# A two-block transformer layer on one core: modulation rows summed along the free axis on VectorE instead of across partitions on GpSimd

## The chip, the core and the metric

The kernel runs on one core of a Trainium2 chip. The engines are TensorE (PE: matmuls; PEld: its weight loads), VectorE (DVE), ScalarE (ACT), GpSimd (POOL) and SyncE (SP), which issues all DMAs of this kernel, in order, from one queue. The metric is the device time of one execution, in microseconds (us).

## The reference

A sequence of 256 tokens with 1024 features goes through two blocks in float32. The first has a hybrid attention mixer, a memory attention and a SwiGLU feed-forward (FFN, 2816 wide); the second is a block whose two norms are modulated by a conditioning vector c:

```python
mod = silu(c) @ w_ada + b_ada                 # c: 1 x 1024, w_ada: 1024 x 6144
shift_m, scale_m, gate_m, shift_f, scale_f, gate_f = split(mod, 6)
h = rms(x) * (1 + scale_m) + shift_m
x = x + gate_m * (mixed(h @ w_in) @ w_out)    # forgetting attention and retention
h = rms(x) * (1 + scale_f) + shift_f
x = x + gate_f * (relu(h @ w_mlp_in)**2 @ w_mlp_out)
```

Block 1 is, in short, `h += merged @ w_out`, where `merged` sums three gated up-projections; `h += memory_attention(h)`; `h += swiglu(rmsnorm(h))`; and a final norm. All six rows of `mod` depend on c alone, so they can be worked out at any time before block 2 needs them.

## The kernel before

**Products.** Every weight comes in tiles of 128x1024 float32 (512 KB; a tile `raw` takes one slot of a pool of 37). ACT rounds it to a high part `wh`, VectorE makes the low part `wl = raw - wh`, and TensorE adds three products of high and low parts in PSUM (`ps`). Activations are brought into the transposed layout as `aT` (or `hT`), by ACT for the high part and VectorE for the low part. In the merge, `mg` is the sum of gated up-projections and `mgt` a gated summand.

**Order.** The whole program is first recorded as operations, then a planner (`Plan`) with a cost for each operation lists them engine by engine in the order in which its model finds them ready; that order is fixed in the program, and each engine runs its own list in order. All instructions are issued from one helper, so they all bear its line, L646 (L634 in the changed kernel); rows are told apart by tile names. The planner's model knows GpSimd's software library: an all-reduce and the other GpSimd work need different ones, and going from one to the other costs `RELOAD`.

**Modulation.** `modulation()` makes s = silu(c) as a 128x8 tile: feature p*8+j lies in partition p, column j. `mod_part(q)` works out half a row of `mod` (512 columns), for q from 0 to 11: GpSimd clears an accumulator `mod` (128x512), a DMA puts 512 values of b_ada into its partition 0, four DMAs bring 512 KB of w_ada each (as `raw`), VectorE does eight products, accumulator += raw times column j of s (`mod_s` in the rows); GpSimd's `partition_all_reduce` sums over the 128 partitions; for the two scale rows VectorE adds 1; a DMA stores 512 values in a DRAM tile `mod_rows`. `mod(i)` later reads row i back, broadcast to all partitions, as `modrow`.

Four parts are started between the products of the merge (`MODG`), six between the groups of the FFN (`MODF`), two in the second block's MLP. Five rows are read back near the FFN's end, the last in the MLP.

The root of a norm is a power on GpSimd, a tensor_tensor of `s` with `mhalf`; `xn` on VectorE, the normed input, waits for it.

Of the kernel before, what the change touches and what calls it, by code (L numbers as in the profile page):

```python
# [16 lines left out]
ALU = mybir.AluOpType  # L17
# [3 lines left out]
P = 128  # L21
S = 256
NT = 2
DM = 1024
# [83 lines left out]
CUTS = ((0, 512, 1024), (0, 512, 768, 1024))  # L108
PIECES = ((0, 256, 512, 1024), (0, 256, 512, 768, 1024))
PIECES0 = ((0, 256, 512, 1024), (0, 512, 1024))  # L110
HORIZON, WINDOW, RELOAD = 30.0, 140, 6.5
TUNING = [
    (1.5, 8.0, 0.1, 5.0, (('qc', 1), ('va_qb', 2))),
    (1.5, 8.0, 0.0, 1.0, (('stick', 8),)),
# [159 lines left out]
class Plan:  # L274
# [146 lines left out]
    @staticmethod  # L421
    def cost(o, views):
        if not views:
            return 1.29
        n = max(math.prod(v.shape[1:]) for v in views)
        psum = any(v.root.kind == "ps" for v in views)
        if o.eng == "pe":
            if o.name == "transpose":
                return 0.11
            n, dt = math.prod(o.args[0].shape[1:]), o.args[1].dtype  # L430
            one = max(0.109, n / 600) if dt == F32 else max(0.054, n / 2250)
            return one * (0.6 if dt == F32 and o.args[0].shape[0] in (32, 64) else 1.0) + 0.0043
        if o.eng == "act":
            return (0.051 if psum else 0.094) + n / 1200 + 0.093 * (isinstance(o.kw.get("scale"), View)
                                                                    + isinstance(o.kw.get("bias"), View) + ("accum_out" in o.kw))
        if o.eng == "dve":
            if o.name == "reciprocal":
                return 0.07 + 0.0062 * n
            fast = not psum and o.name in ("tensor_copy", "tensor_scalar")
            small = o.name in ("tensor_scalar", "scalar_tensor_tensor") and len(views) > (2 if fast else 3)  # L440
            return 0.068 + n / (1920 if fast else 960) + 0.06 * small
        if o.eng == "pool":
            if o.name == "partition_all_reduce":
                return 3.57
            if o.name == "memset":
                return 0.035 + n / 1200
            if ALU.pow in o.args:
                return 0.3 + 0.165 * n
            return 0.15 + n * (0.0034 if o.name == "tensor_scalar" else 0.0031 if o.name == "tensor_copy" else 0.0021)
        return Plan.moved(o)  # L450
# [42 lines left out]
    def begin(self):  # L493
        s = State()
# [5 lines left out]
        s.left = [len(o.pred) for o in self.ops]  # L500
        s.form, s.start, s.end = ([None] * len(self.ops) for _ in range(3))
        s.avail = {e: [] for e in self.HOP}
        s.order, s.library = [], False
        s.clock["pool"] = 8.3
        for o in self.ops:
            if not o.pred:
                self.offer(s, o)
# [2 lines left out]
    def offer(self, s, o):  # L510

        for f in o.forms:
# [2 lines left out]
                e = s.form[q.i][0]  # L515
                at = max(at, s.end[q.i] + self.LAG[e].get(f[0], self.LAG[e][None]))
            s.avail[f[0]].append((o, f, at))

    @staticmethod
    def foreign(s, name):  # L520

        return name != "memset" and (name == "partition_all_reduce") != s.library

    def run(self, s, keys, wait, patience, stop):

# [21 lines left out]
        while len(s.order) < len(ops) and s.dense < stop:  # L547
            best = None
            for e, av in s.avail.items():
                t0 = max(s.clock[e], s.now)  # L550
                cand = []
                for c in av:
                    o, f, ready = c
                    at = room(o, e, t0)
                    if e == "pool" and at is not None and self.foreign(s, f[1]):
                        at = max(at, s.clock[e] + RELOAD)
                    if at is None:
                        continue
                    t = max(t0, ready, at)
# [20 lines left out]
                continue  # L580
            t, e, (o, f, _) = best
            i = o.i
            if e == "pool" and self.foreign(s, f[1]):
                s.library = not s.library
            s.start[i], s.form[i] = t, f
            for r in o.roots:
                if r.kind in todo and s.slot[r.i] is None:
# [61 lines left out]
class Net:  # L649
# [1048 lines left out]


    def modulation(self):  # L1700
        nc, a = self.nc, self.a
        self.mod_w = a["w_ada_2"].rearrange("(p j) n -> p j n", p=P)
        self.mod_rows = self.tile("dram", DM, nm="mod_rows")[0:6]
        c, s = (self.fixed(8, f"mod_{n}") for n in "cs")
        nc.sync.dma_start(c, a["c_2"].rearrange("a (p j) -> (a p) j", p=P))
        nc.vector.tensor_scalar(s, c, -80.0, None, ALU.max)
        nc.scalar.activation(s, s, AF.Exp, scale=-1.0)
        nc.vector.tensor_scalar(s, s, 1.0, None, ALU.add)
        nc.vector.reciprocal(s, s)
        nc.vector.tensor_tensor(s, s, c, ALU.mult)  # L1710
        self.mod_c = s

    def mod_part(self, q):

        nc = self.nc
        c0 = q * 512
        acc = self.k(2, [P, 512], nm="mod")
        nc.gpsimd.memset(acc, 0.0)
        nc.sync.dma_start(acc[0:1, :], self.a["b_ada_2"][:, c0:c0 + 512])
        for j0 in range(0, 8, 2):  # L1720
            raw = self.k(4, [P, 1024], nm="raw")
            r = raw.rearrange("p (k n) -> p k n", k=2)
            nc.sync.dma_start(r, self.mod_w[:, j0:j0 + 2, c0:c0 + 512])
            yield
            for j in range(2):
                nc.vector.scalar_tensor_tensor(acc, r[:, j, :], self.mod_c[:, j0 + j:j0 + j + 1], acc, ALU.mult, ALU.add)
        yield
        nc.gpsimd.partition_all_reduce(acc, acc, channels=P, reduce_op=bass_isa.ReduceOp.add)
        if q // 2 in (1, 4):
            yield  # L1730
            nc.vector.tensor_scalar(acc, acc, 1.0, None, ALU.add)
        yield
        nc.sync.dma_start(self.mod_rows[q // 2:q // 2 + 1, c0 % DM:c0 % DM + 512], acc[0:1, :])

    def next_part(self):
        if not self.mod_parts:
# [407 lines left out]
def views(aps):  # L2144

    out = {}
    for k, ap in aps.items():
        if k in ("b_ada_2", "c_2", "norm_final", "const_a", "const_b"):
            out[k] = ap
        else:  # L2150
            out[k] = ap[0]
    return out


# [17 lines left out]
```

## Time and profile before

| | |
|---|---|
| Time, median of 3 runs | 784.13 us (782.67 to 786.28) |
| Profiled execution | 782.47 us |
| Its span in the profile | 780.7 us |
| TensorE busy | 751.6 us (96%) |
| VectorE busy | 603.6 us (77%) |
| ACT busy | 395.6 us (51%) |
| GpSimd busy | 95.4 us (12%) |
| Read from HBM | 159.22 MB, 205 GB/s over the span |

The span reaches from the first to the last instruction; the time of an execution has some 1.8 us more. Busy means that an instruction runs; a busy TensorE can run at the full clock (granted clock 1.00) or at half of it (0.50). "Idle before" is the time an engine stood still ahead of an instruction, with what released it. SPq is SP's DMA queue.

### The profile page before, as it was taken

How to read it: one execution, taken by the hardware profiler on the slowest of the kernel's cores; microseconds unless marked ns; L12 is line 12 of the kernel's file. 1: busy time of each engine (PE TensorE's matmuls, PEld its weight loads, DVE VectorE, ACT ScalarE, POOL GpSimd, SP SyncE). 2: the span in 40 equal slices, each digit the busy share in tenths (PEclk: the TensorE clock that was granted, in tenths of full speed). 3: DMA queues.
4: the chain of work that ended last, by engine and by line, in shares of the span. 5: the costliest groups of instructions: out<-in, count | busy, mean ns of one | idle time of the engine just before them, and what ended most of it. 6: DMA issues, size and time to landing. Idle time of an engine off the chain costs nothing. (4 is left out here: it accounts for less than half of the span.)

```text
span 780.7 us, 13305 instructions
## 1 busy us (share of the span) xinstructions
PE 751.6 (96%) x5195; PEld 683.7 (88%) x5195; DVE 603.6 (77%) x933; ACT 395.6 (51%) x652; POOL 95.4 (12%) x75
## 2 busy tenths in 40 slices
PE   5999999997998999999999899999999999999998
PEld 4978899996897999999999678798887999999996
DVE  5999989989589997877827788889769997555522
ACT  6684774346278645333326464663536535544510
POOL 0112002411000112222200122020101021000000
PEclk9999999998999999999999999999999999999999
DMA  9828475957366686788788576635427886555401
GB/s 315 268 82 256 157 234 186 362 211 248 135 213 226 210 276 230 239 283 268 243 291 253 151 211 161 142 108 195 156 82 270 288 299 236 188 181 187 159 1 55
DMA packets 92019, 161.17 MB, mean 206 GB/s; under 512 B 6227, under 2 KB 42227, under 8 KB 91956
## 3 DMA queue, kind: packets, MB, share of 16 engines
q1 hardware_dynamic: 91956, 160.32, 62.5%
q8 instruction: 41, 0.67, 0.4%
q14 instruction: 22, 0.18, 0.1%
HBM read 159.22 MB, written 1.07 MB: 205 GB/s over the span
## 5 line engine op out<-in xcount | busy, mean ns | idle before, releaser
L646 DVE TENSOR_TENSOR wl<-raw,wh 128x1024 fp32r<-128x1024 f32 (+4 forms) x237 | 298.5, 1289 | 65.5 <-ACT wh L646 55.2
L646 ACT ACTIVATE wh<-raw 128x1024 fp32r<-128x1024 f32 (+4 forms) x237 | 243.1, 1042 | 161.4 <-DMA raw<-in_w_ffn_out_dram 30.5
L646 PE MATMUL ps<-aT,wh 128*128 128x256 f32 x1664 | 307.1, 284 | 0.6 <-ACT silu L646 0.6
L646 PEld LDWEIGHTS ps<-aT,wh 128*128 128x128 f32 x1664 | 258.1, 189 | 2.0 <-issue 1.0
L646 PE MATMUL ps<-aT,wl 128*128 128x256 f32 x832 | 236.1, 284 | 0.0
L646 PE MATMUL ps<-wh,aT 128*128 128x512 f32 (+5 forms) x672 | 185.1, 360 | 7.1 <-ACT aT L646 5.2
L646 PEld LDWEIGHTS ps<-aT,wl 128*128 128x128 f32 x832 | 157.1, 189 | 0.1
L646 PE MATMUL ps<-wh,hT 128*128 128x512 f32 (+1 forms) x540 | 142.1, 352 | 3.0 <-ACT hT L646 2.4
L646 PEld LDWEIGHTS ps<-wh,aT 128*128 128x128 f32 x672 | 120.2, 192 | 24.8 <-ACT aT L646 5.9
L646 PE MATMUL ps<-wl,aT 128*128 128x512 f32 (+5 forms) x336 | 118.6, 357 | 0.0
L646 PEld LDWEIGHTS ps<-wh,hT 128*128 128x128 f32 x540 | 94.8, 190 | 18.2 <-ACT hT L646 2.9
L646 PE MATMUL ps<-wl,hT 128*128 128x512 f32 (+1 forms) x270 | 94.8, 351 | 0.0
L646 DVE SCALAR_TENSOR_TENSOR mod<-raw,mod_s,mod 128x512 f32<-128x512 f32 x96 | 71.9, 749 | 6.5 <-DMA raw<-in_w_ada_dram 5.0
L646 POOL PARTITION_ALL_REDUCE mod<-mod x12 | 49.0, 4080 | 218.5 <-DVE mod L646 218.5
L646 PEld LDWEIGHTS ps<-wl,aT 128*128 128x128 f32 x336 | 64.2, 191 | 7.4
L646 PEld LDWEIGHTS ps<-wl,hT 128*128 128x128 f32 x270 | 51.2, 190 | 7.2
L646 POOL TENSOR_TENSOR s<-s,mhalf 128x1 f32<-128x1 f32 (+3 forms) x22 | 24.3, 1108 | 224.3 <-DVE s L646 215.0
L646 ACT ACTIVATE junk<-x 128x512 f32<-128x512 f32 (+1 forms) x29 | 16.1, 554 | 37.5 <-DVE x L646 36.0
L646 DVE TENSOR_TENSOR relu<-relu 128x512 f32<-128x512 f32 x16 | 12.9, 820 | 23.3 <-ACT relu L646 23.1
L646 PE MATMUL ps<-ident,xn 128*128 128x128 f32 x96 | 19.4, 313 | 7.0 <-DVE xn L646 5.6
L646 ACT ACTIVATE relu<-ps 128x512 f32<-128x512 f32 x16 | 9.4, 597 | 29.3 <-PE ps L646 28.7
L646 DVE TENSOR_TENSOR aT<-ps,aT 128x256 fp32r<-128x256 f32 (+1 forms) x41 | 20.2, 515 | 4.0 <-ACT aT L646 3.8
(280 smaller groups left out, 654.1 us busy)
## 6 DMA issues: line engine op xcount, KB each, us to landing
raw<-in_w_in_dram SPq DMA_DIRECT2D x62, 512.0 KB, 6.7
raw<-in_w_ada_dram SPq DMA_DIRECT2D x48, 512.0 KB, 5.5
raw<-in_w_ffn_in_dram SPq DMA_DIRECT2D x44, 512.0 KB, 6.4
raw<-in_w_mlp_in_dram SPq DMA_DIRECT2D x32, 512.0 KB, 3.5
raw<-in_w_mlp_out_dram SPq DMA_DIRECT2D x32, 512.0 KB, 4.9
raw<-in_w_ffn_out_dram SPq DMA_DIRECT2D x22, 512.0 KB, 4.2
raw<-in_w_out_dram SPq DMA_DIRECT2D x16, 512.0 KB, 3.7
raw<-in_w_up_dram SPq DMA_DIRECT2D x6, 512.0 KB, 5.7
```

The source lines that it names most:

```text
L646: getattr(get[o.eng], name)(*map(real, args), **{k: real(v) for k, v in kw.items()})
```

## The change

The transposed w_ada (6144 x 1024) is made on the host and passed in. An output of the modulation now lies in a partition, and the sum over the 1024 features runs along the row, on VectorE alone: s goes to a row of DRAM and is read back, broadcast to all partitions, as `mod_c` (128x1024, held in one of the 37 slots to the end). A part loads four tiles of 128x1024 (contiguous rows) and does one product of 128x1024 for each, written in place, with the sum along the row in one column of `mod_s`. After each second part one addition of 128x8 adds b_ada (loaded once as `mod_b`, 128x48) and, for the scale rows, 1; a DMA stores the 1024 values. The accumulators, their clearing, their bias DMAs and the all-reduces are gone, and from the planner what it knew of GpSimd's libraries. In all 96 products of 128x512 become 48 of 128x1024, 12 all-reduces and 12 clearings go, 12 bias loads and 12 stores become one bias load and 6 stores, and the turn of s through DRAM comes in.

```diff
-HORIZON, WINDOW, RELOAD = 30.0, 140, 6.5
+HORIZON, WINDOW = 30.0, 140
...
-            if o.name == "partition_all_reduce":
-                return 3.57
...
-        s.order, s.library = [], False
-        s.clock["pool"] = 8.3
+        s.order = []
...
-    @staticmethod
-    def foreign(s, name):
-
-        return name != "memset" and (name == "partition_all_reduce") != s.library
...
-                    if e == "pool" and at is not None and self.foreign(s, f[1]):
-                        at = max(at, s.clock[e] + RELOAD)
...
-            if e == "pool" and self.foreign(s, f[1]):
-                s.library = not s.library
...
     def modulation(self):
+
         nc, a = self.nc, self.a
-        self.mod_w = a["w_ada_2"].rearrange("(p j) n -> p j n", p=P)
-        self.mod_rows = self.tile("dram", DM, nm="mod_rows")[0:6]
-        c, s = (self.fixed(8, f"mod_{n}") for n in "cs")
+        self.mod_w = a["w_ada_2"].rearrange("(i p j) k -> i p j k", i=6, p=P)
+        self.mod_rows = self.tile("dram", DM, nm="mod_rows")[0:7]
+        self.mod_b, self.mod_s = self.fixed(48, "mod_b"), self.fixed(48, "mod_s")
+        nc.sync.dma_start(self.mod_b.rearrange("p (i j) -> p i j", i=6),
+                          a["b_ada_2"].rearrange("a (i p j) -> (a p) i j", i=6, p=P))
+        c, s = (self.small(8, f"mod_{n}") for n in "cs")
         nc.sync.dma_start(c, a["c_2"].rearrange("a (p j) -> (a p) j", p=P))
...
-        self.mod_c = s
+        nc.sync.dma_start(self.mod_rows[6:7, :].rearrange("a (p j) -> (a p) j", p=P), s)
+        self.mod_c = self.k(4, [P, DM], nm="mod_c")
+        nc.sync.dma_start(self.mod_c, self.mod_rows[6:7, :].to_broadcast([P, DM]))
 
     def mod_part(self, q):
 
         nc = self.nc
-        c0 = q * 512
-        acc = self.k(2, [P, 512], nm="mod")
-        nc.gpsimd.memset(acc, 0.0)
-        nc.sync.dma_start(acc[0:1, :], self.a["b_ada_2"][:, c0:c0 + 512])
-        for j0 in range(0, 8, 2):
-            raw = self.k(4, [P, 1024], nm="raw")
-            r = raw.rearrange("p (k n) -> p k n", k=2)
-            nc.sync.dma_start(r, self.mod_w[:, j0:j0 + 2, c0:c0 + 512])
-            yield
-            for j in range(2):
-                nc.vector.scalar_tensor_tensor(acc, r[:, j, :], self.mod_c[:, j0 + j:j0 + j + 1], acc, ALU.mult, ALU.add)
+        i = q // 2
+        for j in range(q % 2 * 4, q % 2 * 4 + 4):
+            raw = self.k(4, [P, DM], nm="raw")
+            nc.sync.dma_start(raw, self.mod_w[i, :, j, :])
+            yield
+            nc.vector.scalar_tensor_tensor(raw, raw, 1.0, self.mod_c, ALU.mult, ALU.mult,
+                                           accum_out=self.mod_s[:, i * 8 + j:i * 8 + j + 1])
         yield
-        nc.gpsimd.partition_all_reduce(acc, acc, channels=P, reduce_op=bass_isa.ReduceOp.add)
-        if q // 2 in (1, 4):
-            yield
-            nc.vector.tensor_scalar(acc, acc, 1.0, None, ALU.add)
-        yield
-        nc.sync.dma_start(self.mod_rows[q // 2:q // 2 + 1, c0 % DM:c0 % DM + 512], acc[0:1, :])
+        if q % 2:
+            s, b = (m[:, i * 8:i * 8 + 8] for m in (self.mod_s, self.mod_b))
+            nc.vector.scalar_tensor_tensor(s, s, 1.0 if i in (1, 4) else 0.0, b, ALU.add, ALU.add)
+            yield
+            nc.sync.dma_start(self.mod_rows[i:i + 1, :].rearrange("a (p j) -> (a p) j", p=P), s)
...
+def EXTRA(given):
+
+    return {"w_ada_2": np.ascontiguousarray(given["w_ada_2"][0].T)}
```

The planner finds another order with these operations. Three places, before and after.

The end of the merge, on VectorE, before: the norm of the memory (`xn_2176`, `xn_2192` from `mx`) stands among the products of the third and fourth part, each of which has its "+1" (TENSOR_SCALAR mod).

```order
L646 SCALAR_TENSOR_TENSOR xn_2176<-mx_1954,s_2050,gain_1942 128x512 x2
L646 SCALAR_TENSOR_TENSOR xn_2192<-mx_1967,s_2155,gain_1942 128x512 x2
L646 SCALAR_TENSOR_TENSOR mod_1629<-raw_1983,mod_s_1307,mod_1629 128x512
L646 SCALAR_TENSOR_TENSOR mod_1629<-raw_2004,mod_s_1307,mod_1629 128x512
L646 TENSOR_SCALAR mod_1200<-mod_1200 128x512
L646 SCALAR_TENSOR_TENSOR mod_1629<-raw_2004,mod_s_1307,mod_1629 128x512
L646 TENSOR_TENSOR wl_2238<-raw_2036,wh_2135 128x1024
L646 SCALAR_TENSOR_TENSOR mod_1629<-raw_2014,mod_s_1307,mod_1629 128x512 x2
L646 TENSOR_TENSOR wl_2273<-raw_2082,wh_2159 128x1024
L646 TENSOR_TENSOR wl_2290<-raw_2132,wh_2185 128x1024
L646 TENSOR_TENSOR wl_2304<-raw_2198,wh_2240 128x1024
L646 TENSOR_SCALAR mod_1629<-mod_1629 128x512
```

And after, with the last products of the four parts ahead of the norm:

```order
L634 SCALAR_TENSOR_TENSOR raw_1965,mod_s_1649<-raw_1965,mod_c_1399 128x1024
L634 SCALAR_TENSOR_TENSOR raw_1985,mod_s_1649<-raw_1985,mod_c_1399 128x1024
L634 SCALAR_TENSOR_TENSOR raw_1995,mod_s_1649<-raw_1995,mod_c_1399 128x1024
L634 TENSOR_SCALAR s_2173<-s_2024 128x1
L634 SCALAR_TENSOR_TENSOR mod_s_1649<-mod_s_1649,mod_b_181 128x8
L634 TENSOR_TENSOR wl_2178<-raw_1915,wh_2046 128x1024
L634 SCALAR_TENSOR_TENSOR xn_2194<-mx_1940,s_2033,gain_1927 128x512 x2
L634 SCALAR_TENSOR_TENSOR xn_2210<-mx_1948,s_2173,gain_1927 128x512 x2
L634 TENSOR_TENSOR wl_2226<-raw_2031,wh_2106 128x1024
L634 TENSOR_TENSOR wl_2240<-raw_2067,wh_2138 128x1024
L634 TENSOR_TENSOR wl_2260<-raw_2133,wh_2170 128x1024
L634 TENSOR_TENSOR wl_2272<-raw_2166,wh_2214 128x1024
```

What moved: nine products and two additions over 512 columns stood between the merge sums and the splits of w_out; now there are four products (the first of them ahead of these rows) and one addition over 8 columns, and all of them stand ahead of xn.

On SP, about the same place, before: two stores of modulation rows stand among the w_out weights.

```order
L646 DMA raw_2198<-in_w_up_dram 128x2x512
L646 DMA raw_2205<-in_w_out_dram 128x1024
L646 DMA mod_rows_1759<-mod_1200 1x512
L646 DMA raw_2236<-in_w_out_dram 128x1024
L646 DMA raw_2268<-in_w_out_dram 128x1024
L646 DMA raw_2306<-in_w_out_dram 128x1024
L646 DMA mod_rows_1759<-mod_1629 1x512
L646 DMA raw_2339<-in_w_out_dram 128x1024
L646 DMA raw_2347<-in_w_out_dram 128x1024
L646 DMA raw_2374<-in_w_out_dram 128x1024
```

And after:

```order
L634 DMA raw_2166<-in_w_up_dram 128x2x512
L634 DMA mod_rows_1332<-mod_s_1649 128x8
L634 DMA raw_2187<-in_w_out_dram 128x1024
L634 DMA raw_2207<-in_w_out_dram 128x1024
L634 DMA raw_2243<-in_w_out_dram 128x1024
L634 DMA raw_2290<-in_w_out_dram 128x1024
L634 DMA raw_2303<-in_w_out_dram 128x1024
L634 DMA raw_2311<-in_w_out_dram 128x1024
L634 DMA raw_2348<-in_w_out_dram 128x1024
```

What moved: one store stands ahead of the first w_out weight, and none among the seven that follow. On GpSimd three libraries were loaded here before (one between the all-reduces and the norm's powers, one back, one on again); after, the powers follow ordinary work.

The end of the FFN, on SP, before: five rows are read behind the last store, then the constants of block 2.

```order
L646 DMA raw_4603<-in_w_ffn_in_dram 128x4x256
L646 DMA mod_rows_1759<-mod_4060 1x512
L646 DMA modrow_4651<-mod_rows_1759 128x1024
L646 DMA modrow_4657<-mod_rows_1759 128x1024
L646 DMA modrow_4663<-mod_rows_1759 128x1024
L646 DMA modrow_4670<-mod_rows_1759 128x1024
L646 DMA modrow_4675<-mod_rows_1759 128x1024
L646 DMA prefix_4681<-in_const_b_dram 128x256
L646 DMA cos_936_4686<-in_const_b_dram 128x256
L646 DMA sin_937_4691<-in_const_b_dram 128x256
L646 DMA cosT_4699<-in_const_b_dram 128x256
L646 DMA raw_4706<-in_w_ffn_in_dram 128x4x256
```

And after:

```order
L634 DMA raw_4437<-in_w_ffn_in_dram 128x4x256
L634 DMA raw_4455<-in_w_ffn_in_dram 128x4x256
L634 DMA mod_rows_1332<-mod_s_1649 128x8
L634 DMA modrow_4496<-mod_rows_1332 128x1024
L634 DMA modrow_4502<-mod_rows_1332 128x1024
L634 DMA modrow_4508<-mod_rows_1332 128x1024
L634 DMA modrow_4514<-mod_rows_1332 128x1024
L634 DMA modrow_4520<-mod_rows_1332 128x1024
L634 DMA raw_4530<-in_w_ffn_in_dram 128x4x256
L634 DMA raw_4562<-in_w_ffn_in_dram 128x4x256
L634 DMA raw_4607<-in_w_ffn_in_dram 128x4x256
L634 DMA prefix_4622<-in_const_b_dram 128x256
```

What moved: the store comes three ffn_in weights sooner, and of these three stand behind the row reads, ahead of the constants.

The start, on VectorE, before: the first splits of the first weight (452 and 904 columns) and the first norm.

```order
L646 TENSOR_SCALAR s_96<-s_83 128x1
L646 TENSOR_TENSOR wl_106<-raw_79,wh_102 128x452
L646 TENSOR_SCALAR s_121<-s_111 128x1
L646 TENSOR_TENSOR wl_132<-raw_86,wh_123 128x904
L646 SCALAR_TENSOR_TENSOR xn_144<-x_68,s_96,ps_90 128x256
L646 SCALAR_TENSOR_TENSOR xn_144<-x_68,s_96,ps_100 128x512
L646 SCALAR_TENSOR_TENSOR xn_144<-x_68,s_96,ps_90 128x256
```

And after:

```order
L634 TENSOR_SCALAR s_99<-s_83 128x1
L634 SCALAR_TENSOR_TENSOR xn_110<-x_68,s_99,ps_90 128x256
L634 SCALAR_TENSOR_TENSOR xn_110<-x_68,s_99,ps_103 128x512
L634 SCALAR_TENSOR_TENSOR xn_110<-x_68,s_99,ps_90 128x256
L634 TENSOR_TENSOR wl_131<-raw_79,wh_106 128x452
L634 TENSOR_SCALAR s_142<-s_115 128x1
L634 TENSOR_TENSOR aT_147<-ps_118,aT_134 128x2x128
L634 TENSOR_TENSOR aT_147<-ps_138,aT_134 128x2x128
L634 SCALAR_TENSOR_TENSOR xn_158<-x_68,s_142,ps_90 128x512
L634 SCALAR_TENSOR_TENSOR xn_158<-x_68,s_142,ps_103 128x512
L634 TENSOR_TENSOR wl_177<-raw_86,wh_152 128x904
```

What moved: the three xn of the first 128 tokens stand ahead of both wl, the wl of 904 columns behind the second norm.

## Rows read from the trace of the kernel before

**Rows 1.** The page's head: the span.

```profile
span 780.7 us, 13305 instructions
```

**Rows 2.** The span cut into stretches: start and end, length, then the busy time (and instructions) of PE, PEld, DVE, ACT and POOL, the granted TensorE clock (1.00 is full speed), the DMA share and GB/s.

```profile
20.00:180.00 160.00, 159.06 (x1279) 148.65 (x1278) 149.57 (x314) 96.50 (x198) 31.16 (x28) 1.00 0.64 214
100.00:149.10 49.10, 49.10 (x419) 47.56 (x418) 45.82 (x93) 27.39 (x66) 8.24 (x2) 1.00 0.73 241
180.00:200.00 20.00, 15.01 (x89) 13.09 (x88) 19.30 (x25) 11.31 (x14) 0.00 (x0) 0.83 0.78 263
260.00:418.00 158.00, 158.00 (x1201) 151.64 (x1201) 122.55 (x128) 64.16 (x73) 26.80 (x12) 1.00 0.80 267
418.00:440.00 22.00, 18.39 (x97) 15.27 (x97) 12.68 (x14) 10.83 (x16) 0.96 (x1) 0.92 0.82 206
```

**Rows 3.** The same view of two short stretches, the first after each of two pauses of TensorE.

```profile
191.37:195.73 4.36, 4.36 (x10) 3.15 (x11) 4.23 (x7) 3.47 (x5) 0.00 (x0) 0.50 0.62 199
434.66:438.08 3.42, 3.42 (x9) 2.65 (x9) 0.52 (x1) 0.00 (x0) 0.00 (x0) 0.50 0.87 317
```

**Rows 4.** TensorE's timeline, three rows: start, duration, operation, in brackets the idle time before it and what ended it.

```profile
191.37 1.52 PE L646 MATMUL ps<-wh,aT 128*128 128x512 f32 x2 [4.99 <-ACT aT L646]
...
419.18 0.50 PE L646 MATMUL ps<-aT,wh 128*128 128x256 f32 x2 [0.62 <-ACT silu L646]
...
433.08 0.50 PE L646 MATMUL ps<-wh,hT 128*128 128x512 f32 x1 [2.41 <-ACT hT L646]
```

**Rows 5.** VectorE's timeline between the first mg of the last merge stage and the mgt that the first w_out product needs.

```profile
149.16 1.28 DVE L646 SCALAR_TENSOR_TENSOR mg<-gT,ps 128x512 f32<-128x512 f32 x2
...
181.17 8.03 DVE L646 TENSOR_TENSOR wl<-raw,wh 128x1024 fp32r<-128x1024 f32 x7
189.11 0.68 DVE L646 SCALAR_TENSOR_TENSOR mgt<-gT,ps 128x512 f32<-128x512 f32 x1
```

**Rows 6.** VectorE's instructions grouped by shape (count, busy us, mean ns, idle time before them): five groups of the stretch 149.9 to 189.05; the modulation products of 85 to 149.1; the wl that ran from 125.2 to 128.2; and the durations (least, median, greatest, ns) of the wl's of 120 to 180.

```profile
L646 DVE TENSOR_TENSOR wl<-raw,wh 128x1024 fp32r<-128x1024 f32 x13 | 17.2, 1373 | 0.0
L646 DVE SCALAR_TENSOR_TENSOR mod<-raw,mod_s,mod 128x512 f32<-128x512 f32 x9 | 6.9, 763 | 0.1
L646 DVE SCALAR_TENSOR_TENSOR xn<-mx,s,gain 128x512 f32<-128x512 f32 x4 | 2.7, 748 | 2.9 <-POOL s L646 2.9
L646 DVE TENSOR_SCALAR mod<-mod 128x512 f32<-128x512 f32 x2 | 0.8, 418 | 0.0
L646 DVE TENSOR_SCALAR s<-s 128x1 f32<-128x1 f32 x2 | 0.4, 208 | 0.4 <-ACT junk L646 0.4
...
L646 DVE SCALAR_TENSOR_TENSOR mod<-raw,mod_s,mod 128x512 f32<-128x512 f32 x23 | 17.2, 747 | 0.5
...
L646 DVE TENSOR_TENSOR wl<-raw,wh 128x1024 fp32r<-128x1024 f32 x1 | 3.3, 3265 | 0.0
...
L646 DVE TENSOR_TENSOR wl<-raw,wh x16: 1210/1217/3269, 119.6 to 177.3; 128x1024 fp32r<-128x1024 f32 x16
```

**Rows 7.** GpSimd's timeline from 118 to 190, four rows, and its all-reduces over the whole span as the page groups them (count, busy us, mean ns, idle before).

```profile
124.01 4.11 POOL L646 PARTITION_ALL_REDUCE mod<-mod  x1 [37.39 <-DVE mod L646]
...
151.20 4.13 POOL L646 PARTITION_ALL_REDUCE mod<-mod  x1 [10.59 <-DVE mod L646]
164.67 1.12 POOL L646 TENSOR_TENSOR s<-s,mhalf 128x1 f32<-128x1 f32 x2 [9.34 <-issue]
173.20 4.11 POOL L646 PARTITION_ALL_REDUCE mod<-mod  x1 [7.42 <-DVE mod L646]
...
L646 POOL PARTITION_ALL_REDUCE mod<-mod x12 | 49.0, 4080 | 218.5 <-DVE mod L646 218.5
```

**Rows 8.** SP's timeline from 150 to 186 (the time is that of issuing, runs of alike DMAs in one row), and what SP waited for from 150 to 182: sum, times, longest.

```profile
169.85 0.25 SPq L646 DMA_DIRECT2D mod_rows<-mod  x1
170.19 1.28 SPq L646 DMA_DIRECT2D raw<-in_w_out_dram  x3
178.88 0.24 SPq L646 DMA_DIRECT2D mod_rows<-mod  x1
...
SPq L646 <- DVE mod L646: 20.6, 3, 11.9
```

**Rows 9.** What SP waited for from 373 to 405 us (sum, times, longest), and one row of ACT's timeline.

```profile
SPq L646 <- DVE mod L646: 6.3, 2, 5.7
...
SPq L646 <- DMA modrow<-mod_rows: 4.4, 4, 1.8
...
403.50 1.06 ACT L646 ACTIVATE wh<-raw 128x1024 fp32r<-128x1024 f32 x1 [11.89 <-DMA raw<-in_w_ffn_in_dram]
```

**Rows 10.** Four groups of instructions over the whole span, of VectorE and, the last, of ACT: count, busy us, mean ns, idle before.

```profile
L646 DVE SCALAR_TENSOR_TENSOR mod<-raw,mod_s,mod 128x512 f32<-128x512 f32 x96 | 71.9, 749 | 6.5 <-DMA raw<-in_w_ada_dram 5.0
...
L646 DVE SCALAR_TENSOR_TENSOR xn<-x,s,gain 128x256 f32<-128x256 f32 x12 | 5.3, 479 | 0.9 <-POOL s L646 0.9
L646 DVE TENSOR_TENSOR xn<-x,modrow 128x512 f32<-128x512 f32 x5 | 3.3, 684 | 0.0
...
L646 ACT ACTIVATION_READ_ACCUMULATOR junk<-x 128x1 f32 x29 | 5.4, 186 | 0.0
```

**Rows 11.** The start: one row of VectorE's timeline and one of GpSimd's.

```profile
10.38 1.10 DVE L646 TENSOR_TENSOR wl<-raw,wh 128x904 fp32r<-128x904 f32 x1 [2.11 <-ACT wh L646]
...
8.37 1.12 POOL L646 TENSOR_TENSOR s<-s,mhalf 128x1 f32<-128x1 f32 x2 [7.95 <-DVE s L646]
```

More of the change, by code (lines that the diff above doesn't have):

```diff
@@ L2147, in views @@
     for k, ap in aps.items():
-        if k in ("b_ada_2", "c_2", "norm_final", "const_a", "const_b"):
+        if k in ("b_ada_2", "c_2", "w_ada_2", "norm_final", "const_a", "const_b"):
             out[k] = ap
@@ L2162 @@
     given["const_a"], given["const_b"] = CONST_A, CONST_B
+    given.update(EXTRA(given))
     for name, arr in given.items():
```

## The prediction

> **What bounds the kernel now.** I read the page first, then the span cut into stages, then each stage in which TensorE pauses, with its engines' timelines. The page's span is 780.7 us [rows 1]. By stages [rows 2], TensorE is busy without a break where the work is long: 158.00 of 158 us in the FFN, 159.06 of 160 between 20 and 180. There, work taken from another engine is worth nothing in itself; only the pauses can be shortened. Two of them touch the modulation: 180 to 200 us, with 15.01 us busy of 20 at a mean clock of 0.83, and 418 to 440, with 18.39 of 22 at 0.92.
>
> The first pause: the matmul at 191.37, the first of the next product, comes after a pause of 4.99 us (from about 186.4), ended by ACT's aT [rows 4]. Afterwards the granted clock is 0.50 (1.2 instead of 2.4 GHz) until 195.73 [rows 3]; those 4.36 us of work would take 2.18 at the full clock. Together 7.2 us.
>
> What makes aT late? Followed back: aT needs mg, and the mgt that mg needs runs on VectorE at 189.11, at the tail of a row of 7 wl splits (8.03 us) [rows 5]. VectorE hardly rests there: from 149.9 to 189.05 its idle time sums to 3.4 us, 2.9 of it before xn, released by GpSimd's s [rows 6]. GpSimd did nothing for 9.34 us before that s, put down to "issue": its all-reduce of 151.20 ended at 155.33, and s (a power) came only at 164.67 [rows 7]. The library load that stands between the two in GpSimd's order is what I read the gap as. SP shows the other half of it: its stores of two modulation rows, at 169.85 and 178.88, each stand ahead of three w_out weights and wait up to 11.9 us for VectorE's "+1" on that row, so w_out is asked for late [rows 8]. All of it comes from the modulation.
>
> The second pause, end of the FFN: 0.62 and 2.41 us [rows 4], and clock 0.50 from 434.66 to 438.08, which costs 3.42/2 = 1.71 [rows 3]; together 4.7. Its root lies earlier: ACT sat 11.89 us for an ffn_in weight at 403.5, and SP had been held 5.7 us for a modulation row and then read five modulation rows and a string of constants [rows 9].
>
> **The change, part by part.**
>
> VectorE's sums. Before: 96 products of 128x512 at 749 ns, 71.9 us [rows 10]; their like on xn takes 748 [rows 6]. After: 48 of 128x1024 that also sum along the row. No such instruction is in the trace. Width: the same operation on xn takes 479 ns at 256 columns and 748 at 512 [rows 6, 10], so 269 per 256, and 748 + 2 x 269 = 1.29 us at 1024. The sum: ScalarE's row sums end in a separate read of 186 ns [rows 10]; if VectorE pays likewise, 1.47 us. Lower bound: the plain two-source operation wl at 1.21 [rows 6]. Upper: twice two 512-wide ones, 4 x 0.749 = 3.0. I take 1.47, since the nearest row, the same operation, scales to it; then the whole is 48 x 1.47 = 70.6 us, as much as before.
>
> The Trainium skill, *Vector Engine (DVE) Microarchitecture Reference*, section *Points that are easy to get wrong*, says that this instruction with two non-bf16 sources in SBUF runs at half throughput, as both read ports are taken and none is left for accumulator readback. The plain form here has two such sources and takes 749 ns where a plain two-source product of that size takes 684 [rows 10]: without accumulation the trace doesn't bear the rule out, with it no run shows. By the rule the sum would be that of rival C at its lower price, 783.
>
> The all-reduces. 12 at 4.08 us on GpSimd go [rows 7]; GpSimd bounds nothing. But a wl that runs beside an all-reduce takes 3.27 us (one does beside that of 124.01), where the median is 1.22 [rows 6, 7]: 2.05 us of VectorE each.
>
> The first pause, by VectorE's order. Between the mg at 149.2 and the mgt at 189.11 stand 9 products before and 4 after [rows 5, 6]. 9 x 0.763 = 6.9 becomes 4 x 1.47 = 5.9: 1.0. The two "+1" of 418 ns become one addition of 8 columns, some 0.2 by the one-column operation on s [rows 6]: 0.6. The wait for s goes, since no library load is left between: 2.9. The 0.4 before the other s I leave. One slowed wl beside the all-reduce of 173.20: 2.05. Sum 6.6: mgt at about 182.5 instead of 189.1. First matmul came 2.26 after mgt, so aT would be ready at 184.8, ahead of the 186.39 at which TensorE is free. The margin is 1.6 us. The weights must also be there: the store on SP now waits for 8 columns behind the last product and not for an all-reduce, the seven w_out loads follow it in a row, and with SP free some 12 us sooner the 7 splits aren't short of data. So the pause and its slow clock go: **-7.2**. What is late next would be wh and wl of the following weights; from 200 to 418 VectorE has slack (122.55 of 158 us busy in the FFN [rows 2]), which also covers the six parts there up to 35 us.
>
> The second pause. SP is no longer held 5.7 us, and three ffn_in weights stand ahead of the constants instead of one. But the five row reads and their turns through DRAM (4.4 us) stay [rows 9]. All of it gone would be -4.7, nothing 0; with something over half the cause removed I take **-2.8**.
>
> The start. The wl of 904 columns (1.10 us from 10.38, ended by a wait on ACT of 2.11) stands ahead of the first xn before, behind them after [rows 11]. The first transposes can start up to 2 us sooner, though not before GpSimd's power, which came at 8.37. The work behind them still needs the same wl, so most is handed back: **-0.7** (-2.0 to +0.5, should the splits now be late).
>
> The setup. c is made into a row through DRAM, store and broadcast back to back on SP. A like turn for modulation rows costs SP 1.1 to 1.8 us each (4.4 in 4) [rows 9]. It is met at about 85 us, where loads run ahead: **+0.4** (0 to +2.5). A slot of 37 is held for this row throughout, and the bias comes as 768 pieces of 32 bytes once; neither stands on a waiting path, 0.
>
> Sum: -7.2 - 2.8 - 0.7 + 0.4 = -10.3. Against its own time of 782.47 (span plus 1.8) that is 772.2. The median of the runs, 784.13, lies 1.66 above: **773.8**.
>
> **Rivals.**
> B, the gain is eaten by the next wait. VectorE is 19.30 of 20 us busy from 180 to 200 [rows 2], so the matmuls that start sooner may run into splits that are not ready; and the second pause may stay. Then half of the first pause is left (-3.6), the rest nil: 780.5, from 779 to 786. For it: the margin of 1.6 us is small. Against: VectorE itself gains 6.6 us there.
>
> C, slower: the summing product is slow. Should it run at half the rate of the plain form, 2 x 1.29 = 2.57 us; the upper bound is 3.0. With price p, the 12 that stand before mg cost 12p against 17.2 for 23 products now [rows 6], less three slowed wl of 6.2, and VectorE has some 3.2 us of slack from 100 us on [rows 2]; behind mg 4(p - 1.47) more than in my sum. mgt moves by 12p - 26.6 + 4(p - 1.47) - 6.6 = 16p - 39.1. At p = 2.57 that is +2.0, which with the -3.1 of the other terms gives no change (783); at 3.0 it is +8.9, so 789.9. From p = 2.64 on it is slower than before. In the FFN 24 x (3.0 - 1.5) = 36 us would just fill the idle 35. For it: no row shows the form. Against: the plain form's price.
>
> D, the change of order costs somewhere that I don't see: 785 to 790.
>
> **How the numbers follow.** Forecast 0.69, with a range of its own from 768 (second pause gone, start at its best) to 779; B 0.19; C 0.07; D 0.05. From 766 to 783 leaves out D, the slow end of C, the upper part of B and little of the forecast: some 2 in 10. What a measurement here can tell from no change is 0.5%, 3.9 us. Faster: the forecast and a little of B, 0.75; same: the rest of B and the middle of C, 0.15; slower 0.10.
>
> **What would show it.** Right: no gap of TensorE near 186 and a clock of 1.00 from 188 to 196; products of 1.3 to 1.6 us; no wl of 3.3 us; no 9 us gap on GpSimd; SP's waits for modulation rows near nothing; w_out landing early; the pause near 430 shorter. Wrong: products over 2 us; a gap of some us still ahead of aT, ended by wh or wl; or new waits of SP on the rows in DRAM.

## The result and the profile after

The changed kernel takes 762.06 us (761.32 to 762.91, 4 runs), the one before 784.49 in the same comparison: ratio 0.9715, 95% interval 0.9689 to 0.974. The forecast was 773.8, with a range from 766 to 783: the sign was right, and the gain is a little over twice the forecast. The profiled execution took 762.54 us with a span of 760.7, 20.0 less than before [rows 1].

The page after, its head and the three engine rows that changed (busy us, share of the span, count):

```profile
span 760.7 us, 13194 instructions
...
PE 744.8 (98%) x5195; PEld 679.8 (89%) x5195; DVE 571.7 (75%) x936; ACT 395.3 (52%) x652; POOL 42.0 (6%) x50
```

TensorE has the same 5195 matmuls in both traces, so the k-th of one can be set beside the k-th of the other. This table is worked out from the two traces (us):

| matmul | starts before, us | starts after, earlier by | gained since the row above | forecast |
|---|---|---|---|---|
| 558th, the start behind it | 96.51 | 3.98 | 4.0 | 0.7, less 0.4 for the setup |
| 1365th, last ahead of the first pause | 186.11 | 4.31 | 0.3 | 0 |
| 1401st, behind it | 200.36 | 11.68 | 7.4 | 7.2 |
| 3001st, end of the FFN | 417.13 | 12.13 | 0.5 | 0 |
| 3121st, behind the second pause | 443.39 | 18.02 | 5.9 | 2.8 |
| 3411th, block 2's attention | 501.17 | 19.56 | 1.5 | 0 |
| 5195th, the last | 776.68 | 19.87 | 0.3 | 0 |

The first pause came out as forecast, the start and the second pause did not. The stretches of the trace after that answer to [rows 2] (columns as there; the stages now stand some 5 and 12 to 18 us earlier):

```profile
145.00:180.00 35.00, 35.00 (x301) 35.00 (x300) 31.60 (x44) 19.96 (x29) 2.09 (x2) 1.00 0.74 283
...
178.00:200.00 22.00, 22.00 (x122) 18.96 (x122) 16.32 (x22) 8.65 (x14) 0.55 (x1) 1.00 0.55 189
...
406.00:428.00 22.00, 22.00 (x136) 19.61 (x136) 13.50 (x21) 9.33 (x21) 2.62 (x3) 1.00 0.47 131
```

TensorE is busy through both places, at a clock of 1.00. VectorE's groups over the whole span, the splits before, then the splits, the products and the reads of their sums after:

```profile
L646 DVE TENSOR_TENSOR wl<-raw,wh 128x1024 fp32r<-128x1024 f32 x222 | 285.5, 1314 | 61.8 <-ACT wh L646 51.5 <-PE ps L646 9.1
```

```profile
L634 DVE TENSOR_TENSOR wl<-raw,wh 128x1024 fp32r<-128x1024 f32 x222 | 265.5, 1220 | 65.9 <-ACT wh L634 49.5 <-PE ps L634 14.6
L634 DVE SCALAR_TENSOR_TENSOR raw<-raw,mod_c 128x1024 f32<-128x1024 f32 x48 | 57.3, 1218 | 6.8 <-DMA raw<-in_w_ada_dram 6.8
L634 DVE DVE_READ_ACCUMULATOR raw<-raw,mod_c 128x1 f32 x48 | 3.9, 81 | 0.0
```

A product costs 1.218 us, as much as a split of its size and less than the 1.47 assumed; the read of the sum, 0.08, lies beside its end, so that two such products stand 1.145 apart from start to start. The splits lost 20 us in all, with none of their own work changed: 1.314 became 1.220 on average. On VectorE's timeline at the end of the merge (compare [rows 5]) xn comes with no wait; the last split ahead of mgt waits 1.19 us for its wh, which costs nothing, since TensorE comes later still:

```profile
159.24 0.15 DVE L634 SCALAR_TENSOR_TENSOR mod_s<-mod_s,mod_b 128x8 f32<-128x8 f32 x1
159.31 1.22 DVE L634 TENSOR_TENSOR wl<-raw,wh 128x1024 fp32r<-128x1024 f32 x1
160.44 2.73 DVE L634 SCALAR_TENSOR_TENSOR xn<-mx,s,gain 128x512 f32<-128x512 f32 x4
...
178.11 1.23 DVE L634 TENSOR_TENSOR wl<-raw,wh 128x1024 fp32r<-128x1024 f32 x1 [1.19 <-ACT wh L634]
179.25 0.68 DVE L634 SCALAR_TENSOR_TENSOR mgt<-gT,ps 128x512 f32<-128x512 f32 x1
```

### The profile page after: what moved, and what is told of

It is laid out like the page before. It is cut to its first block, busy times and chain, and to the rows that moved or that the text cites. A ratio compares the mean times of both kernels' runs of the same rounds, so it can differ in the third digit from the quotient of the medians.

```text
span 760.7 us, 13194 instructions
## 1 busy us (share of the span) xinstructions
PE 744.8 (98%) x5195; PEld 679.8 (89%) x5195; DVE 571.7 (75%) x936; ACT 395.3 (52%) x652; POOL 42.0 (6%) x50
## 4 chain that ended last, share of the span: by engine, by line
PE 77%; DVE 11%; issue 6%; ACT 2%; DMA 2%; POOL 1%; SPq 0%; POOLq 0%; DVEq 0%; ACTq 0%
PE ps L634 77%; DVE wl L634 3%; DMA raw<-in_w_in_dram 2%; DVE s L634 1%; DVE sc L634 1%; DVE x L634 1%; DVE xn L634 1%; ACT wh L634 1%; DVE rp L634 1%; SPq L634 0%; POOL s L634 0%; DVE mk L634 0%; ACT prob L634 0%; DVE gt L634 0%; DVE aT L634 0%
## 5 line engine op out<-in xcount | busy, mean ns | idle before, releaser
L634 DVE TENSOR_TENSOR wl<-raw,wh 128x1024 fp32r<-128x1024 f32 (+4 forms) x237 | 279.1, 1203 | 66.0 <-ACT wh L634 49.5
L634 PE MATMUL ps<-wh,aT 128*128 128x512 f32 (+5 forms) x672 | 181.8, 357 | 2.1 <-ACT wh L634 1.3
L634 PE MATMUL ps<-wh,hT 128*128 128x512 f32 (+1 forms) x540 | 140.1, 348 | 0.0
L634 PEld LDWEIGHTS ps<-wh,aT 128*128 128x128 f32 x672 | 118.6, 190 | 19.1 <-ACT wh L634 1.9
L634 DVE SCALAR_TENSOR_TENSOR raw<-raw,mod_c 128x1024 f32<-128x1024 f32 x48 | 57.3, 1218 | 6.8 <-DMA raw<-in_w_ada_dram 6.8
L634 DVE TENSOR_TENSOR relu<-relu 128x512 f32<-128x512 f32 x16 | 10.9, 691 | 22.4 <-ACT relu L634 22.2
L634 ACT ACTIVATE prob<-ps,s 128x256 f32<-128x256 f32 (+1 forms) x48 | 20.0, 447 | 9.4 <-DVE s L634 9.4
L634 ACT ACTIVATE hT<-silu 128x512 fp32r<-128x512 f32 x10 | 6.3, 632 | 31.0 <-DVE silu L634 31.0
```

The source lines that it names most:

```text
L634: getattr(get[o.eng], name)(*map(real, args), **{k: real(v) for k, v in kw.items()})
```

## The experiments

Most of the kernels below leave out a part of the modulation's sums or repeat it; only their times are used. The new time has three possible sources: GpSimd's work that went (all-reduces and loads of libraries), the new order, and the other products on VectorE. The first experiments separate these.

**The order before, no all-reduces.** In the kernel before, at the place where instructions are issued:

```diff
+                    if name == "partition_all_reduce":
+                        col = real(args[0])[:, 0:1]
+                        nc.gpsimd.tensor_tensor(col, col, col, ALU.add)
+                        continue
```

> The kernel before with its order on every engine kept, but each all-reduce is replaced on GpSimd by an addition over one column of the accumulator (the sum across partitions is left out), so GpSimd needs one library only. Theory G (GpSimd's all-reduces and library loads caused the pauses, the new order and the wider products did not): the pause of 7.2 us at 186, the one of 5.3 to 5.9 us at 418 to 438 and the 1.4 us near 490 go, the first transposes stay at 11.9 because the split of 904 columns still stands ahead of xn: about 769 us, 767 to 771. Rival O (the new order and the shorter products brought most of it): one of the two large pauses stays, 775 or more; if the pause at the end of the FFN stays, 775, if the one at 186 stays, 777.

Measured: 769.15 us, ratio 0.982 (0.9782 to 0.9859). The trace: both pauses gone, the first transposes at 11.96.

```profile
178.00:200.00 22.00, 22.00 (x138) 19.75 (x138) 17.48 (x21) 9.14 (x12) 0.00 (x0) 1.00 0.70 240
404.00:426.00 22.00, 22.00 (x152) 20.32 (x151) 11.04 (x13) 9.27 (x12) 0.96 (x1) 1.00 0.78 199
```

By matmuls, the first pause gives 7.4 us and the second 6.0, just as in the changed kernel. So neither the new order nor the new products are needed for either; the all-reduces made both pauses. The 1.5 us near 490 us, which I had put down to them too, did not come: they belong to the new order. The start did not move either.

**The start.** The changed kernel with an all-reduce (0.9 us on the 128x48 sums) as GpSimd's last instruction, and the same with an ordinary addition behind it:

```diff
+            s = real(self.last_rows)
+            nc.gpsimd.partition_all_reduce(s, s, channels=P, reduce_op=bass_isa.ReduceOp.add)
...
```
```diff
...
+            nc.gpsimd.tensor_tensor(s[:, 0:1], s[:, 0:1], s[:, 0:1], ALU.add)
...
```

> The changed kernel with one all-reduce of 128x48 as GpSimd's last instruction, so that an execution ends with the all-reduce's library loaded, as before the change. Theory L (the library that the execution before left is what the first power waits for): GpSimd's first operation starts at about 8.4 us instead of 5.05, the first transposes at 9.5 to 11 instead of 7.7, and the time is 1.4 to 3 us longer, 763.5 to 765; all behind the start unchanged. Rival O (the order at the start alone, xn ahead of the splits, brought the 4 us): GpSimd starts at 5.05, 762.

> The run above with one ordinary addition on GpSimd behind the all-reduce, so that the execution ends with the ordinary library. Theory L: the start is that of the changed kernel again, GpSimd's first operation at 5.05 us, 762. Rival (a program that holds an all-reduce anywhere pays a load at its start): first operation at 8.4, 763.5 to 765.

Measured: 764.27 and 762.40 us. GpSimd's timeline at the start: the changed kernel, then the one with the all-reduce at its end, then the one with the addition behind it:

```profile
5.05 0.43 POOL L634 TENSOR_TENSOR both<-ident 128x16 f32<-128x16 f32 x2 [4.61 <-DMA ident<-in_const_a_dram]
5.48 0.55 POOL L634 TENSOR_TENSOR s<-s,mhalf 128x1 f32<-128x1 f32 x1
```

```profile
8.30 0.39 POOL L634 TENSOR_TENSOR both<-ident 128x16 f32<-128x16 f32 x2 [7.87 <-issue]
8.65 0.59 POOL L634 TENSOR_TENSOR s<-s,mhalf 128x1 f32<-128x1 f32 x1
```

```profile
5.31 0.43 POOL L634 TENSOR_TENSOR both<-ident 128x16 f32<-128x16 f32 x2 [4.88 <-DMA ident<-in_const_a_dram]
5.70 0.59 POOL L634 TENSOR_TENSOR s<-s,mhalf 128x1 f32<-128x1 f32 x1
```

What matters is which library the execution before left behind: with the all-reduce's, GpSimd stands still until 8.30, and the first transposes come at 9.81 instead of 7.67. With the run above, the four cases of the start are complete: in the old order the transposes come at 11.92 with the load (GpSimd's power at 8.37, [rows 11]) and 11.96 without, in the new one at 9.81 and 7.67. In the old order the load costs nothing, since the split of 904 columns at 10.4 keeps xn back anyway; the new order brings 2.1 us, and only then does the load's absence bring 1.8 more (kept to the 558th matmul).

**How much room VectorE has.** Each product issued twice, and each as two of 512 columns:

```diff
+                    for _ in range(2 if "accum_out" in kw and o.eng == "dve" and name == "scalar_tensor_tensor" else 1):
...
```
```diff
...
+                        for h in (slice(0, 512), slice(512, 1024)):
+                            nc.vector.scalar_tensor_tensor(out[:, h], raw[:, h], 1.0, c[:, h], ALU.mult, ALU.mult,
+                                                           accum_out=real(kw["accum_out"]))
...
```

> The changed kernel with each of the 48 summing products issued twice in a row, in the same place (the second works on the result of the first, so the modulation rows are others). It adds 48 x 1.15 = 55 us to VectorE. Theory: only the four products between the mg sums and the mgt of the last merge stage reach TensorE, as the pause there has no margin left (mgt at 179.25, the next product's first matmul at 182.15 after a gap of 0.34): 4 x 1.15 = 4.6 us later, and 1.5 to 2.3 more if the clock falls to 0.50; the FFN hides its 24. 767 to 770. Rival (VectorE has room everywhere): 762 to 763.

> The changed kernel with each summing product of 128x1024 issued as two of 128x512, in the same place (the column keeps the sum of the second half alone, so the modulation rows are others). The question is whether VectorE's saving of some 15 us over the products of before (57.3 against 71.9 us) is part of the gain. At 0.68 + 0.08 each it adds some 0.3 us a tile, 15 in all, 1.2 of them between the mg sums and the mgt. Theory (the saving isn't needed): 762 to 763.5. Rival (VectorE's room is what made the pauses go): one of the pauses at 182, 370 to 405 or 418 comes back, 765 or more.

Measured: 793.46 us for the products twice, 762.77 for the halves (0.69 us each and 0.08 for the read; VectorE is busy 578.6 us instead of 571.7). So giving 7 us of the saving on the products back costs next to nothing, and the first run had shown that both pauses go with the old products too. But twice the products cost 31 us where I expected 5 to 8. The new pauses don't stand where I expected them, ahead of mgt, but earlier; TensorE's timeline:

```profile
158.06 0.58 PE L635 MATMUL ps<-aT,wh 128*128 128x256 f32 x1 [5.75 <-DVE mg L635]
...
177.86 0.45 PE L635 MATMUL ps<-ident,xn 128*128 128x128 f32 x1 [4.43 <-DVE xn L635]
```

From 145 to 180 VectorE is 34.23 of 35 us busy there. The FFN, where VectorE idles 54 us in the changed kernel (104.09 of 158 busy between 260 and 418), did not hide 28 us more: its matmuls fell 10 us further behind. I read it so: the products come in bunches ahead of splits, and a bunch has to fit into the room at its place.

**Libraries, length, slowed splits or waits?** In my first theory the loads of libraries made the first pause and the wait for the all-reduce's end the second. Three multiplications of 128x512 in place of each all-reduce (long, no second library), and the all-reduce cut to one column (short, all the loads):

```diff
...
+                        for _ in range(3):
+                            nc.gpsimd.tensor_tensor(acc, acc, acc, ALU.mult)
...
```
```diff
...
+                        args = [real(v)[:, 0:1] for v in args]
```

> The kernel before, order kept, with each all-reduce replaced by three ordinary multiplications of 128x512 on GpSimd (some 3.9 us together, as long as an all-reduce of 4.08; no second library). Theory (the loads of libraries make the pause at 186, the length of the all-reduce, by SP's wait for it, the one at the FFN's end): the pause at 186 is gone, the one of 418 to 438 is there: 773 to 776. Rival (library loads make both): 769 as without the all-reduces. Rival (length and the slowed splits make both): 780 or more.

> The kernel before, order kept, with each all-reduce cut to one column of the accumulator (some 0.6 to 0.9 us instead of 4.08; the other columns stay unsummed), so that all the library loads stay and the length goes. Theory as above: the pause at 186 stays for the most part (9 us without GpSimd ahead of the norm's powers, xn waits), the one of 418 to 438 goes: 774 to 778. Rival (length makes both): 769 to 771. Rival (library loads make both): 782 or more.

Measured: 784.80 us (ratio 1.0036) and 768.82 (0.9803). The theory falls: without libraries both pauses are there, with them and short all-reduces neither is. In the short run the program still changes libraries ahead of the norm's powers, but nothing waits for it: the row says that the power waited for VectorE's s.

```profile
160.02 1.65 POOL L648 TENSOR_TENSOR s<-s,mhalf 128x1 f32<-128x1 f32 x2 [9.55 <-DVE s L648]
```

The multiplications took longer than meant, 5.4 us on average for three, so this run bears harder than the all-reduces; it shows that length is enough, not by which way.

Length can act in three ways: splits beside it are slowed; what needs its sum waits; and the norm's powers, which stand behind it on GpSimd, come later, as in [rows 7]. The next two runs were meant to part the first two. The short all-reduce followed by a full one on a scratch tile that nobody reads; and, in its place, two powers of 128x8, long and with few bytes:

```diff
...
+                        col = real(args[0])[:, 0:1]
+                        nc.gpsimd.partition_all_reduce(col, col, **kw)
+                        args = (self.scratch, self.scratch)
...
```
```diff
...
+                        acc = real(args[0])[:, 0:8]
+                        for _ in range(2):
+                            nc.gpsimd.tensor_tensor(acc, acc, self.zeros, ALU.pow)
...
```

> The kernel before, order kept, with each all-reduce cut to one column of the accumulator (1.3 us, for which the store and the additions wait) and followed by an all-reduce of 128x512 on a scratch tile (4.1 us) that nobody reads. So the splits on VectorE are slowed as before, 2.05 us each time, and nothing of the modulation waits for the long part; only the norm's powers, which stand behind it on GpSimd, do. Theory C (the slowed splits make the pauses, as VectorE is short of time there): both pauses come back, 778 to 783. Theory W (the waits for the all-reduce's end, by SP's store and VectorE's additions, make them): 769 to 771, as with the short ones alone.

> The kernel before, order kept, with each all-reduce replaced by two powers of 128x8 on GpSimd on the accumulator (2.09 us each in the trace of before, 4.2 together, few bytes, no second library). So the store and the additions wait as long as before and the splits beside it should not be slowed. Theory C: 769 to 771. Theory W: 778 to 783. One pause back and the other gone (774 to 777) would put them down to different causes.

Measured: 778.43 us (0.9911, 0.9876 to 0.9946) and 773.38 (0.9855). The profiled execution of the second took 768.34, the other four 773 to 774.5; it was measured again beside the kernel without all-reduces, and with four powers:

> The run without the all-reduces again, as the neighbour of the two below on the same chip: 769 us, no pause at 186 and none at 418 to 438.

> The run with the waits of 4.2 us and no slowed splits again, since its timed executions lay at 773 to 774 and the profiled one at 768.3. Theory C (the waits alone cost little): within 2 us of its neighbour without them. Theory W2 (the waits bring a part of a pause back in most executions): 3 to 6 us above its neighbour, and a profile taken in such an execution shows TensorE waiting near 182 or 418 to 438.

> The same with four powers instead of two, so waits of 8.4 us instead of 4.2 and still no slowed splits. Theory C: at most some 4 us more, in one place (what the waits still cost is the time by which they pass the slack), no return of both pauses: 769 to 775. Theory W2: both pauses as long as before or longer, 782 or more.

Measured: 768.20, 772.78 and 795.21 us, with ratios to before of 0.9809, 0.9862 and 1.0155. The splits of the whole span, slowed in the first of the two and not in the second:

```profile
L650 DVE TENSOR_TENSOR wl<-raw,wh 128x1024 fp32r<-128x1024 f32 x222 | 280.8, 1292 | 65.0 <-ACT wh L650 55.7 <-PE ps L650 7.9
```

```profile
L651 DVE TENSOR_TENSOR wl<-raw,wh 128x1024 fp32r<-128x1024 f32 x222 | 265.4, 1222 | 62.9 <-ACT wh L651 53.5 <-PE ps L651 8.2
```

The first pause on TensorE's timeline, with slowed splits, with waits of 4.5 us (two powers), and with waits of 8.2:

```profile
192.80 0.79 PE L650 MATMUL ps<-wh,aT 128*128 128x512 f32 x1 [5.80 <-ACT aT L650]
```

```profile
187.70 0.49 PE L651 MATMUL ps<-wh,aT 128*128 128x512 f32 x1 [1.00 <-ACT aT L651]
```

```profile
192.07 0.80 PE L651 MATMUL ps<-wh,aT 128*128 128x512 f32 x1 [5.56 <-ACT aT L651]
```

What each gains against before at the two pauses, in one profiled execution each, by matmuls 1365 to 1401 and 3001 to 3121 (minus is a loss). "Sum" is the mean time on GpSimd for which the store and the additions wait, "s" VectorE's wait ahead of xn:

| kernel (old order but the last) | splits slowed | sum, us | s, us | libraries | first pause | second pause | time, us |
|---|---|---|---|---|---|---|---|
| before | yes | 4.1 | 2.9 | two | 0 | 0 | 784 |
| slowed, sum not waited for | yes | 1.2 | 2.8 | two | -0.4 | 3.1 | 778.4 |
| multiplications | yes | 5.4 | 0 | one | 0.3 | 0.0 | 784.8 |
| powers | no | 4.5 | 0 | one | 6.8 | 6.0 | 773.4 (profiled 768.3) |
| powers again | no | 4.5 | 0 | one | 5.6 | 4.4 | 772.8 (profiled 771.7) |
| powers twice | no | 8.2 | 0 | one | -1.4 | -0.5 | 795.2 |
| short all-reduces | no | 1.3 | 0 | two | 7.4 | 6.0 | 768.8 |
| none | no | 1.0 | 0 | one | 7.4 | 6.0 | 769.2 |
| changed | no | none | 0 | one | 7.4 | 5.9 | 762.1 |

Loads of libraries behind short all-reduces cost nothing. Waits for the sums alone bring back between nothing and a quarter of either pause, 4.6 of 15.0 us by the medians; only when doubled do they bring back all (and then pause the FFN in between as well, hence 795 us). The expectation that they would stay within 2 us of their neighbour missed, and so did that of at most 4 us more when doubled.

The run with slowed splits brings back the whole first pause, but not by the splits alone: as in the kernel before, GpSimd's powers came late there, and VectorE waited for them.

```profile
165.51 1.12 POOL L650 TENSOR_TENSOR s<-s,mhalf 128x1 f32<-128x1 f32 x2 [9.25 <-issue]
```

```profile
166.14 2.74 DVE L650 SCALAR_TENSOR_TENSOR xn<-mx,s,gain 128x512 f32<-128x512 f32 x4 [2.82 <-POOL s L650]
```

What VectorE's time is made of can be added up, as it runs the same list from the last two sums mg to mgt in all kernels of the old order. It takes 24.54 us there with short all-reduces (mgt at 182.94) and 29.57 before (189.11): of the 5.0 us between them 2.90 are the wait for s and 2.05 one slowed split, and mg itself came 1.1 later. In the run with slowed splits 2.82 and 2.05 come in, and mg is 2.1 later. The multiplications have no wait for s: two slowed splits cost 1.7 there, the additions with their wait 1.2, and mg is 3.3 later, with four splits slowed ahead of it. So slowed splits and the late s made the first pause together; without the late s some 2.1 of its 4.99 us would have been left (an estimate, 4.99 less 2.90). No run has the slowed splits alone there.

At the second pause the run does part them: GpSimd has no powers from 335 to 440 us, and two slowed splits and a slowed addition, with a short wait for the sum, bring back about half, 2.9 of 6.0 us. How the rest comes about, beyond these rows, is open. At both places VectorE is the late one.

## Why the prediction was right and wrong

**The first pause (7.2 forecast, 7.4 measured).** Time and mechanism hold, the exact sum was partly luck. The two terms that carry it, 2.9 us of waiting for s and one slowed split of 2.05, are what VectorE lost before between mg and mgt, and both are gone. I had put the wait down to the library's load; the short all-reduces, which keep the load, show that it delays s only behind a long all-reduce. The terms for products and additions (1.6) were not needed: with the old ones the pause goes as well. And I had left out of this sum the two splits slowed ahead of mg (at 124.92 and 137.43), as I took mg to be set by TensorE; with short all-reduces the first mg comes at 147.0 instead of 149.2. In all mgt came 9.9 us sooner, 5.6 of them gained on TensorE where I had 6.6. The margin of 1.6 us was small indeed: with the 2.26 us of [rows 4, 5], aT was ready in the changed kernel 0.4 us before TensorE, which came at 181.91.

**The second pause (2.8 forecast, 5.9 measured).** The failed step is its root: "ACT sat 11.89 us for an ffn_in weight at 403.5, and SP had been held 5.7 us for a modulation row and then read five modulation rows and a string of constants". I took something over half because the row reads stay. In the first run with powers SP is held as long at the FFN's end, and the pause is gone; with the short all-reduces ACT sits as long for its weight, and the pause is gone too. What SP waited for from 365 to 410 us in the one, and ACT's row in the other:

```profile
SPq L651 <- DVE mod L651: 5.8, 1, 5.8
```

```profile
387.28 1.06 ACT L648 ACTIVATE wh<-raw 128x1024 fp32r<-128x1024 f32 x1 [11.88 <-DMA raw<-in_w_ffn_in_dram]
```

Against before ACT's wait ends 16.2 us sooner there, TensorE's FFN only 7.4. So neither wait was the root; it was the long all-reduces, about half of it by what they slow on VectorE, and all of it goes with them. I also left out the 0.58 us that follows the 2.41 us pause.

**The start (0.7 forecast, 4.0 measured).** Two steps failed. "Most is handed back": it is not, as TensorE is the bound from there on (159.06 of 160 us, [rows 2]); the 2.1 us that the order brings at the first transposes are there at the 558th matmul still. And "not before GpSimd's power, which came at 8.37": I read the load at the start as fixed because its instruction stands in both programs; but it was slow only because the execution before had ended with the other library.

**The rest.** The setup's turn through DRAM cost nothing that can be seen (forecast +0.4): between the 422nd and 558th matmul the changed kernel gained. The 1.5 us in block 2's attention are the new order's, for which I had no term there. VectorE makes two `rnat` ahead of the keys of that attention before (at 485.95 and 486.60), and one after, the other being GpSimd's (467.03, 4.00 us); whether that is the reason was not tried. A term of 0.9 us between the 1752nd and 1900th matmul comes and goes between two profiles of one kernel, and one of 1.2 near 453 us stands in some kernels' profiles and not in others. Last, I had added 1.66 us because the median lay above the profiled execution; after the change it lies 0.48 below, which is 2.1 of the 11.7 us by which the forecast missed.

**Rival C and the price of the product.** The product costs 1.22 us, below every bound of mine but the lowest (1.21). By the Trainium skill's *Vector Engine (DVE) Microarchitecture Reference*, section *Points that are easy to get wrong*, it should run at half throughput; here it runs at a plain split's pace, and the measurement decides. The rival's arithmetic was wrong as well: it put the point where the kernel is slower than before at 2.64 us, while two products of 1.145 (start to start) already give 793 us. It counted VectorE's idle time in the FFN as cover, which it is not, and looked for the loss ahead of one mgt only.

**Slowed splits, as the skill tells them.** The Trainium skill's *SBUF — State Buffer*, section *SBUF: two separate sides*, says that GpSimd and VectorE share a port pair by an exclusive lock, and that between a VectorE instruction with two SBUF inputs and a GpSimd one that reads SBUF the first to start has it for the whole instruction. Splits and all-reduces do collide as it says, but a split that began 0.9 us into an all-reduce of 4.1 lost 2.05 us [rows 6, 7], not the 3.2 that were left of it (GpSimd's spans are rough in the profile), and the powers of 2.2 us, which read SBUF too, slowed no split by a measurable amount (1222 ns on average).

## What to carry to other kernels

Where an engine other than the bound one is short of time just ahead of a pause, look for what slows its instructions, not only for what it waits for: a group whose greatest duration is far above its median (1217 and 3269 ns here) points to a neighbour. Here the long GpSimd instructions made both pauses, 13.3 of the 20 us, by slowing splits beside them and by holding up GpSimd's own next work; the waits for their sums were the smaller part. When such an instruction is moved or stretched to test it, see what stands behind it on its own engine: the run that was to show slowed splits alone delayed the norm's powers too. And an idle sum over a stage is no cover for work that comes in bunches: test it by doing the work twice.

## What the runs showed of the hardware

GpSimd's library outlives the execution: with the all-reduce's library left behind, the next execution's first GpSimd operation came at 8.30 us, otherwise at 5.05 to 5.31. All runs fit this: in the four kernels whose last GpSimd instruction is an all-reduce the first operation came at 8.30 to 8.91, in the others at 5.05 to 5.75. VectorE's product with a sum along the row costs 1.218 us for 128x1024 float32, the same as the plain two-source operation, and a read of the sum 0.08. Three GpSimd multiplications of 128x512 slowed VectorE's splits by 15.5 us in all, nearly as much as the all-reduces' 20.
